# Half of the gated head outputs turned by transposing transfers instead of TensorE

## The chip, the cores and the metric

The kernel runs on one core of one Trainium2 chip. The metric is the device time of one execution in microseconds (us); lower is better. The time before is the median of three runs.

## What is computed

One layer of a hybrid decoder trunk for 512 tokens of 1024 channels, in float32. The part that matters here is branch B, a gated linear attention with 4 heads of 256 value channels, and its output gate:

```python
o = _gla_chunked(qh, kh, vh, gkh)                    # 512 tokens x 4 heads x 256
o = o * lax.rsqrt(jnp.mean(o * o, axis=-1, keepdims=True) + EPS) * gla_norm_g[l]
o = o.reshape(bsz, seq, GLA_VDIM) * jax.nn.silu(r)   # r = u @ (a part of w_in), 1024 wide
y_gla = o @ w_gla_out[l]
merged = jax.nn.sigmoid(gate_a) * y_conv + jax.nn.sigmoid(gate_b) * y_gla
```

The heads leave o with tokens on the partitions. The product with w_gla_out needs o with channels on the partitions, so the gated o, 512 tokens by 1024 channels of float32, has to be transposed.

## The kernel before

Every large product is made of three matmuls (lines 541 to 543, `mm3`): each operand is split into a high part and a low part, and low x high, high x low and high x high are added up in one PSUM bank. ScalarE (ACT) makes the high part of a weight (`whi`, line 426 or 456) and VectorE (DVE) the low part (`wlo`, line 427 or 464). Weights come as tiles of 512 KB into four `raw` buffers. SyncE's queue (SP) issues nearly all of these loads, in an order that is fixed when the program is built, and each load waits until the buffer it overwrites has been read. Tokens come in four tiles p of 128; channels of o in two halves n of 512 (two heads each) or in eight tiles m of 128.

Every engine works through its own list in order. A scheduler builds the lists from the program text and its own estimates, so an instruction that waits holds up everything behind it on its engine.

The stretch around the change has four pieces, in this order.

1. *The heads.* Class `Head` leaves the normalised output in `ot[p, n]` (called `h` in the trace), 128 tokens x 512 channels.
2. *The product for r.* `seven("w_r", ...)` computes u @ w_r by the seven-product scheme of Strassen and Winograd, in the steps a11, a12, s1, n2, s4, n3, a22, each with two products of 24 matmuls in all. Four of the steps complete two blocks (p, n) each: a12 blocks (0,0) and (1,0); s4 blocks (0,1) and (1,1); n3 blocks (2,1) and (3,1); a22 blocks (2,0) and (3,0). `put_r` applies the silu on ACT (line 1555 or 1550) into a tile `r`, and DVE then multiplies `ot[p, n]` by it (line 1561, the last one at 1565), one block late.
3. *The turning.* `gated_o(m, bank)` (lines 1246 to 1259) turns one channel tile: four TensorE transposes of 128x128 (line 1250) into one PSUM bank `ax`, one ACT instruction that scales it into the high part (line 1257), one DVE instruction that makes the low part (line 1258). Their results are `oa[m]`; tiles m = 0 to 3 are called `oa` in the trace and 4 to 7 `h`. The eight calls come in pairs: (4,5) at the end of the product for r, (6,7), (0,1) and (2,3) inside the next piece.
4. *Gate B, tiles 6 and 7.* `two_tiles` (lines 1344 to 1382) makes two column tiles of gate B at once, in four quarters x1, x3, x2, x4 of 24, 24, 24 and 12 matmuls 256 wide. A sum of weight pieces for x3 and x4 is made on GpSimd (POOL, `two_sums`, line 398). The quarters accumulate into three banks x, y and z, and after a part of the sum is complete ACT copies it out (line 1351) before the next quarter goes on in the same bank. So x3 cannot begin on bank x before ACT has copied what x1 left there. The pairs of turned tiles stand after x1, x3 and x2. Behind x4 comes the product with w_gla_out (`tile_of("w_gla", m, ...)`), which needs all eight `oa`.

Of the kernel before, what the change touches and what calls it, by code (L numbers as in the profile page):

```python
# [12 lines left out]
BF16 = mybir.dt.bfloat16  # L13
U8 = mybir.dt.uint8
AF = mybir.ActivationFunctionType
ALU = mybir.AluOpType

P = 128
D = 1024
T = 512  # L20
# [80 lines left out]
def trunk_layer(ctx: ExitStack, tc: tile.TileContext, a: dict, out: bass.AP):  # L101
# [15 lines left out]
    tp = pool("temps", 1)  # L117
    ps = pool("psum", 1, bass.MemoryType.PSUM)
    edge = ctx.enter_context(tc.tile_pool(name="edge", bufs=1, side="right"))
    heap_scope, hp = scoped("heap", 26)  # L120
# [9 lines left out]
    def heap(dt=F32):  # L130
        return hp.tile([P, T], dt, tag="h", name=nm("h"))
# [143 lines left out]
    ready, raws = [], []  # L275
    pair_raws = {}
    kept = {}
# [136 lines left out]
    def split_weight(halves=False, between=None):  # L414

        if len(ready) < len(order):
# [4 lines left out]
            if name in SEVEN or name == "two":  # L421
# [3 lines left out]
                lo = wp.tile([P, D], F32R, tag="wlo", name=nm("wlo"), bufs=4)[:, :n]  # L425
                nc.scalar.copy(hi, raw)  # L426
                two_low[:] = [nc.vector.tensor_tensor(lo, raw, hi.bitcast(F32), ALU.subtract)]  # L427
# [817 lines left out]

    def gated_o(m, bank):
        po = bank()
        c = (m % 4) * P
        for p in range(NT):
            nc.tensor.transpose(po[:, p * P : (p + 1) * P], ot[p, m // 4][:, c : c + P], ident)  # L1250
        gain = pp[:, PP_GG + m % 2 : PP_GG + m % 2 + 1]
        if m < 3:
            both = tp.tile([P, 2, T], F32R, tag="x", name=nm("oa"), bufs=3)
        elif m == 3:
            both = tp.tile([P, 2, T], F32R, tag="gain", name=nm("oa"), bufs=1)
        hi, lo = (both[:, 0, :], both[:, 1, :]) if m < 4 else (heap(F32R), heap(F32R))
        nc.scalar.activation(hi, po, AF.Copy, scale=gain)
        low_at[:] = [nc.vector.scalar_tensor_tensor(lo, po, gain, hi.bitcast(F32), ALU.mult, ALU.subtract)]
        oa[m] = hi, lo

# [279 lines left out]
    def sums_for(step):  # L1540
        while urgent and step in ("s1", "n2", "s4", "n3") and step not in merge_acts:
            urgent.pop(0)[1]()

    def put_r(step, t, n, acc):
        if step in ("a11", "s1", "n2"):
            rt[t, n] = rp_.tile([P, T], F32, tag="r", name=nm("r"), bufs=6)
            return nc.scalar.copy(rt[t, n], acc)
        if step == "a22":
            rt[t, n] = rp_.tile([P, T], F32, tag="r", name=nm("r"), bufs=6)
            nc.scalar.activation(rt[t, n], acc, AF.Silu)  # L1550
        else:
            r = rt[t, n]
            one, two = (r, acc) if step == "n3" else (acc, r)
            done = nc.vector.tensor_tensor(r, one, two, ALU.add if step == "a12" else ALU.subtract)
            nc.scalar.activation(r, r, AF.Silu)
        if step == "a22":
            done = None
        with tc.issue_after(done.ins) if done else ExitStack():
            while gated:
                i, j = gated.pop()  # L1560
                nc.vector.tensor_tensor(ot[i, j], ot[i, j], rt[i, j], ALU.mult)
        gated.append((t, n))
        if (step, t, n) == ("a22", 3, 0):
            i, j = gated.pop()
            nc.vector.tensor_tensor(ot[i, j], ot[i, j], rt[i, j], ALU.mult)
        return done if step == "n3" else None

    def r_at(step, i):
        if (step, i) == ("a22", 1):
            for m in range(4, 6):  # L1570
                gated_o(m, ax_bank)

    seven("w_r", R_PAIRS, [ByTile(k) for k in range(4)], None, r_at, put=put_r, before=sums_for)
    half_of = [range(KT // 2), range(KT // 2, KT)]
# [4 lines left out]
    def pair_7(n):  # L1579
# [5 lines left out]
        for j in range(4):  # L1585
# [6 lines left out]
            if n == 0 and j < 3:  # L1592
                for m in ((6, 7), (0, 1), (2, 3))[j]:
                    gated_o(m, ax_bank)
                if j == 2:
                    start_norms()
# [425 lines left out]
```

## Time and profile before

| | |
|---|---|
| median of the three runs | 817.39 us (817.36 to 818.07) |
| the profiled execution, its own time | 816.96 us |
| its span in the trace | 815.3 us |
| TensorE (PE) busy | 807.5 us, 99% |
| VectorE, ScalarE, GpSimd busy | 700.7, 487.9, 192.5 us |
| the 32 transposes of line 1250 | start at 284.2 to 296.2 us |
| the eight scalings of line 1257 on ScalarE | 284.9 to 297.1 us, about 0.68 us each |
| the eight low parts of line 1258 on VectorE | 286.5 to 298.9 us, about 0.74 us each |

In a row of the trace the first number is the start in us from the span's start, the second the duration, then engine, line, operation, and the tiles as written tile <- read tiles. A name in brackets at the end is what ended the engine's idle time before it. Instructions of one engine overlap a little at their ends, so the distance between two starts is less than the duration. SPq is the queue of SyncE, where a transfer is issued; the time that a transfer takes until its data has landed is given with the DMA issues.

### The profile page before, as it was taken

How to read it: one execution, taken by the hardware profiler on the slowest of the kernel's cores; microseconds unless marked ns; L12 is line 12 of the kernel's file. 1: busy time of each engine (PE TensorE's matmuls, PEld its weight loads, DVE VectorE, ACT ScalarE, POOL GpSimd, SP SyncE). 2: the span in 40 equal slices, each digit the busy share in tenths (PEclk: the TensorE clock that was granted, in tenths of full speed). 3: DMA queues.
4: the chain of work that ended last, by engine and by line, in shares of the span. 5: the costliest groups of instructions: out<-in, count | busy, mean ns of one | idle time of the engine just before them, and what ended most of it. 6: DMA issues, size and time to landing. Idle time of an engine off the chain costs nothing.

```text
span 815.3 us, 11441 instructions
## 1 busy us (share of the span) xinstructions
PE 807.5 (99%) x4215; PEld 693.2 (85%) x4215; DVE 700.7 (86%) x1108; ACT 487.9 (60%) x746; POOL 192.5 (24%) x166
## 2 busy tenths in 40 slices
PE   9999999999999999999999999999999999999996
PEld 7888888788888898989888898898889988899885
DVE  6679999998998988486779899979976999789896
ACT  6667788677546575494435655556435663466655
POOL 2025433332204332122001100320133300522010
PEclk9999999999999999999999999999999999999999
DMA  8487858745831232432458613145732345334662
GB/s 337 146 198 179 187 160 176 161 119 135 186 95 60 78 130 78 137 105 95 164 124 220 190 57 126 52 154 156 144 127 92 142 117 167 105 104 171 165 129 105
DMA packets 36616, 113.60 MB, mean 139 GB/s; under 512 B 3704, under 2 KB 8960, under 8 KB 36560
## 3 DMA queue, kind: packets, MB, share of 16 engines
q1 hardware_dynamic: 29200, 86.92, 30.8%
q0 software_dynamic: 7200, 25.69, 18.0%
q8 instruction: 33, 0.54, 0.3%
q14 instruction: 23, 0.19, 0.1%
q10 hardware_dynamic: 160, 0.27, 0.1%
HBM read 110.76 MB, written 2.10 MB: 138 GB/s over the span
## 4 chain that ended last, share of the span: by engine, by line
PE 84%; DVE 13%; issue 1%; ACT 1%; DMA 1%; SPq 0%; DVEq 0%; ACTq 0%
PE mm L541 20%; PE mm L542 20%; PE mm L543 20%; DVE c L902 5%; PE cv L541 4%; PE cv L542 4%; PE cv L543 4%; DVE aside L902 3%; PE ax L542 2%; PE ax L541 2%; PE ax L543 2%; PE ax L1230 1%; PE ax L1232 1%; DMA kept<-in_w_r_dram 1%; PE ax L1212 0%
## 5 line engine op out<-in xcount | busy, mean ns | idle before, releaser
L541 PE MATMUL mm<-uh,wlo 128*128 128x512 f32 (+1 forms) x532 | 193.9, 364 | 0.2 <-DVE wlo L464 0.2
L542 PE MATMUL mm<-ul,whi 128*128 128x512 f32 (+1 forms) x532 | 191.6, 360 | 0.0
L543 PE MATMUL mm<-uh,whi 128*128 128x512 f32 (+1 forms) x532 | 191.4, 360 | 0.0
L427 DVE TENSOR_TENSOR wlo<-raw,whi 128x1024 fp32r<-128x1024 f32 x82 | 96.0, 1178 | 36.0 <-ACT whi L426 32.2
L398 POOL TENSOR_TENSOR raw<-raw,raw 128x512 f32<-128x512 f32 x39 | 63.9, 1638 | 236.3 <-DVE wlo L427 130.9
L541 PEld LDWEIGHTS mm<-uh,wlo 128*128 128x128 f32 x532 | 100.5, 189 | 15.6 <-DVE wlo L464 0.6
L543 PEld LDWEIGHTS mm<-uh,whi 128*128 128x128 f32 x532 | 100.4, 189 | 15.4
L542 PEld LDWEIGHTS mm<-ul,whi 128*128 128x128 f32 x532 | 100.5, 189 | 14.7
L426 ACT CAST whi<-raw 128x1024 fp32r<-128x1024 f32 x82 | 78.9, 965 | 41.4 <-PE mm L543 24.4
L456 ACT CAST whi<-raw 128x1024 fp32r<-128x1024 f32 x80 | 83.5, 1048 | 27.5 <-PE mm L543 13.9
L464 DVE TENSOR_TENSOR wlo<-raw,whi 128x1024 fp32r<-128x1024 f32 x50 | 66.3, 1331 | 7.1 <-ACT whi L456 6.8
L426 ACT CAST whi<-kept 128x1024 fp32r<-128x1024 f32 (+1 forms) x40 | 40.1, 1008 | 32.4 <-DVE kept L374 16.5
L902 DVE SCALAR_TENSOR_TENSOR aside<-cv,pp,aside 128x255 f32<-128x255 f32 (+6 forms) x112 | 52.2, 466 | 0.0
L902 DVE SCALAR_TENSOR_TENSOR c<-aside,btmp,c 128x247 f32<-128x247 f32 (+13 forms) x93 | 52.1, 565 | 0.0
L427 DVE TENSOR_TENSOR wlo<-kept,whi 128x1024 fp32r<-128x1024 f32 (+1 forms) x40 | 47.5, 1191 | 4.9 <-ACT whi L426 4.7
L902 DVE SCALAR_TENSOR_TENSOR c<-cv,pp,c 128x247 f32<-128x247 f32 (+13 forms) x93 | 43.2, 465 | 1.4 <-ACT c L898 1.4
L458 ACT ACTIVATE wlo<-raw 128x1024 fp32r<-128x1024 f32 x28 | 29.4, 1059 | 19.1 <-PE mm L541 19.1
L1351 ACT COPY tmp<-mm 128x256 f32<-128x256 f32 x38 | 14.1, 370 | 35.1 <-PE mm L543 34.3
L1733 DVE SCALAR_TENSOR_TENSOR tmp<-mm,pp,tmp 128x511 f32<-128x511 f32 (+1 forms) x42 | 31.2, 743 | 3.5 <-ACT tmp L1730 3.4
L1733 DVE SCALAR_TENSOR_TENSOR tmp<-tmp,pp,tmp 128x511 f32<-128x511 f32 (+1 forms) x32 | 27.8, 888 | 0.3
L1504 DVE TENSOR_TENSOR hres<-hres,mm 128x512 f32<-128x512 f32 (+1 forms) x37 | 24.7, 676 | 2.2 <-PE mm L543 2.1
L542 PE MATMUL cv<-ul,whi 128*128 128x512 f32 (+1 forms) x72 | 25.6, 356 | 0.0
(514 smaller groups left out, 2078.3 us busy)
## 6 DMA issues: line engine op xcount, KB each, us to landing
raw<-in_w_up_dram SPq DMA_DIRECT2D x44, 512.0 KB, 3.2
raw<-in_w_glu_dram SPq DMA_DIRECT2D x16, 512.0 KB, 5.1
raw<-in_w_down_dram SPq DMA_DIRECT2D x16, 512.0 KB, 3.4
wlo<-in_w_glu_dram POOLq DMA_DIRECT2D x12, 512.0 KB, 7.1
kept<-in_w_down_dram POOLq DMA_DIRECT2D x9, 512.0 KB, 5.5
raw<-in_w_v_dram SPq DMA_DIRECT2D x8, 512.0 KB, 6.0
raw<-in_w_qk_dram SPq DMA_DIRECT2D x8, 512.0 KB, 6.3
raw<-in_w_gb_dram SPq DMA_DIRECT2D x8, 512.0 KB, 4.0
```

The source lines that it names most:

```text
L398: work = nc.gpsimd.tensor_tensor(out, x, y, ALU.add)
L426: nc.scalar.copy(hi, raw)
L427: two_low[:] = [nc.vector.tensor_tensor(lo, raw, hi.bitcast(F32), ALU.subtract)]
L456: nc.scalar.copy(hi, raw)
L458: pace[0] = nc.scalar.mul(lo, raw, -1.0)
L464: pace[0] = nc.vector.tensor_tensor(lo, raw, hi.bitcast(F32), ALU.subtract)
L541: nc.tensor.matmul(acc, ll, rh, start=first, stop=False, **kw)
L542: nc.tensor.matmul(acc, lh, rl, start=False, stop=False, **kw)
L543: nc.tensor.matmul(acc, lh, rh, start=False, stop=last, **kw)
L902: nc.vector.scalar_tensor_tensor(out[:, j:], x[:, : half_t - j], w, out[:, j:], ALU.mult, ALU.add)
L1504: done = nc.vector.tensor_tensor(hres[t, n][:, c], hres[t, n][:, c], acc[:, c], op)
L1733: nc.vector.scalar_tensor_tensor(z[:, s:], acc[:, : T - s], w[j], z[:, s:], ALU.mult, ALU.add)
```

## The change

The tokens of tiles p = 0 and 1 (half of the gated o, whose blocks are gated earliest) no longer go through TensorE. When such a block has been gated, ACT copies its 16 bit words, low halves and high halves apart, over the `r` tile that has just been used (`words`), and SP's queue writes them to a buffer in DRAM as rows of 16 bit words, two rows for each token. When both blocks of a half n are written, SP's queue reads them back by a transfer that transposes 16 bit words (`turn_o`): one of 512x512 words for n = 0 and two of 512x256 for n = 1. The two words of a float32 come to lie side by side again, so the landing holds 256 tokens of float32 with channels on the partitions. The landings take the place of a loaded weight (`rx`) and of two `r` tiles.

The transposes of tiles p = 2 and 3 stay on TensorE, two channel tiles to a bank (`gated_two`). The scaling and the low part are now made in halves of 256 tokens (`half_o`), from PSUM for the later tokens and from the landing for the earlier ones. For tiles 4 to 7 the halves out of the landing stand one pair of calls later than those out of PSUM. All these halves are ordered behind the last silu, or behind the low parts of earlier tiles, and the first high parts of gate B's weights are ordered behind the last copied words.

```diff
+    dram = pool("dram", 1, bass.MemoryType.DRAM)
...
-                nc.scalar.copy(hi, raw)
+                with tc.issue_after(behind_planes[0].ins) if behind_planes and spec[0] == "w_gb" else ExitStack():
+                    nc.scalar.copy(hi, raw)
...
-    def gated_o(m, bank):
+    last_silu = []
+    turned, words_of = {}, [dram.tile([T, DV * 2], U16, name=nm("words")) for _ in range(2)]
+
+    def words(t, n):
+
+        planes = rt[t, n].bitcast(U16).rearrange("p (two c) -> p two c", two=2)
+        behind_planes[:] = [nc.scalar.copy(planes, ot[t, n].bitcast(U16).rearrange("p (c two) -> p two c", two=2))]
+        rows = words_of[n][2 * t * P : 2 * (t + 1) * P, :]
+        nc.sync.dma_start(rows.rearrange("(p two) c -> p two c", two=2), planes)
+
+    def turn_o(n):
+        if n == 0:
+            landings = [rp_.tile([P, 4, H], F32, tag="rx", name=nm("turned"), bufs=1)]
+        else:
+            landings = [rp_.tile([P, 2, H], F32, tag="r", name=nm("turned"), bufs=6) for _ in range(2)]
+        many = 4 // len(landings)
+        for i, landing in enumerate(landings):
+            c = slice(i * many * P, (i + 1) * many * P)
+            nc.sync.dma_start(landing.bitcast(U16), words_of[n][:, c], transpose=True)
+            for j in range(many):
+                turned[4 * n + i * many + j] = landing[:, j, :]
+
+    def gated_two(m, bank):
         po = bank()
-        c = (m % 4) * P
-        for p in range(NT):
-            nc.tensor.transpose(po[:, p * P : (p + 1) * P], ot[p, m // 4][:, c : c + P], ident)
-        gain = pp[:, PP_GG + m % 2 : PP_GG + m % 2 + 1]
+        for j in range(2):
+            c = (m % 4 + j) * P
+            for p in (2, 3):
+                at = j * H + (p - 2) * P
+                nc.tensor.transpose(po[:, at : at + P], ot[p, m // 4][:, c : c + P], ident)
+        for j in range(2):
+            start_o(m + j)
+            if m < 4:
+                half_o(m + j, slice(0, H), turned[m + j], last_silu)
+            half_o(m + j, slice(H, T), po[:, j * H : (j + 1) * H], last_silu)
+        if m < 4:
+            for j in range(2):
+                half_o(m + 4 + j, slice(0, H), turned[m + 4 + j], low_at)
...
-        nc.scalar.activation(hi, po, AF.Copy, scale=gain)
-        low_at[:] = [nc.vector.scalar_tensor_tensor(lo, po, gain, hi.bitcast(F32), ALU.mult, ALU.subtract)]
-        oa[m] = hi, lo
+        oa[m] = (both[:, 0, :], both[:, 1, :]) if m < 4 else (heap(F32R), heap(F32R))
+
+    def half_o(m, c, x, behind_op):
+        (hi, lo), gain = oa[m], pp[:, PP_GG + m % 2 : PP_GG + m % 2 + 1]
+        with tc.issue_after(behind_op[0].ins):
+            nc.scalar.activation(hi[:, c], x, AF.Copy, scale=gain)
+            low = nc.vector.scalar_tensor_tensor(lo[:, c], x, gain, hi[:, c].bitcast(F32), ALU.mult, ALU.subtract)
+        if m < 4:
+            low_at[:] = [low]
...
+    def gate_o(t, n):
+        nc.vector.tensor_tensor(ot[t, n], ot[t, n], rt[t, n], ALU.mult)
+        if t < 2:
+            words(t, n)
+        if t == 1:
+            turn_o(n)
...
-                i, j = gated.pop()
-                nc.vector.tensor_tensor(ot[i, j], ot[i, j], rt[i, j], ALU.mult)
+                gate_o(*gated.pop())
         gated.append((t, n))
         if (step, t, n) == ("a22", 3, 0):
-            i, j = gated.pop()
-            nc.vector.tensor_tensor(ot[i, j], ot[i, j], rt[i, j], ALU.mult)
+            gate_o(*gated.pop())
+            gated_two(4, ax_bank)
...
-                for m in ((6, 7), (0, 1), (2, 3))[j]:
-                    gated_o(m, ax_bank)
+                gated_two((6, 0, 2)[j], ax_bank)
```

The program's lists change at two places that matter. The first is ScalarE at the end of the product for r, from the silu of block (1,1) to the high parts of gate B's first two weights. Before:

```order
L1555 ACTIVATE r_2599<-r_2599 128x512
L1555 ACTIVATE r_2545<-r_2545 128x512
L426 CAST whi_2683<-raw_2644 128x1024
L426 CAST whi_2691<-raw_2687 128x1024
L1555 ACTIVATE r_2559<-r_2559 128x512
L1550 ACTIVATE r_2708<-cv_2412 128x512
```

The same place after (the `h` are gated blocks, `r` the used gate tiles, `raw_2656` and `raw_2705` the weights of x1 and x3):

```order
L1603 ACTIVATE r_2605<-r_2605 128x512
L1255 COPY r_2591<-h_2129 128x1024
L1603 ACTIVATE r_2551<-r_2551 128x512
L1255 COPY r_2605<-h_2131 128x1024
L429 CAST whi_2701<-raw_2656 128x1024
L1603 ACTIVATE r_2565<-r_2565 128x512
L429 CAST whi_2709<-raw_2705 128x1024
L1598 ACTIVATE r_2726<-cv_2416 128x512
```

The two copies of words of half n = 1 now stand ahead of both high parts, and one silu stands between these. The second place is ScalarE a little later, from the last silu to the high part of the first weight of w_gla_out. Before:

```order
L1550 ACTIVATE r_2741<-mm_2413 128x512
L1257 ACTIVATE h_2728<-ax_2723,pp 128x512
L426 CAST whi_2800<-raw_2687 128x512
L1257 ACTIVATE h_2737<-ax_2732,pp 128x512
L1351 COPY tmp_2748<-mm_2745 128x256
L456 CAST whi_2848<-raw_2754 128x1024
```

After (`turned_2632` is the landing of the first transposing transfer, `turned_2682` that of the second):

```order
L1598 ACTIVATE r_2741<-mm_2417 128x512
L1297 ACTIVATE h_2750<-ax_2745,pp 128x256
L429 CAST whi_2808<-raw_2705 128x512
L1297 ACTIVATE oa_2845<-turned_2632,pp 128x256
L1297 ACTIVATE oa_2850<-turned_2632,pp 128x256
L1297 ACTIVATE h_2754<-ax_2745,pp 128x256
L1392 COPY tmp_2761<-mm_2758 128x256
L1297 ACTIVATE h_2750<-turned_2682,pp 128x256
L1297 ACTIVATE h_2754<-turned_2682,pp 128x256
L459 CAST whi_2859<-raw_2767 128x1024
```

The copy of x1's sum out of bank x (`tmp_2761<-mm_2758`) now stands behind two halves out of the first landing, and the copies that follow it behind halves out of the second and third. On SP's list the four writes and the three transposing transfers come in among the weight loads. Before, from the loads for gate B on:

```order
L292 DMA raw_2644<-in_w_gb_dram 128x1024
L292 DMA raw_2645<-in_w_gb_dram 128x1024
L296 DMA raw_2754<-in_w_gla_dram 128x1024
L296 DMA raw_2804<-in_w_gla_dram 128x1024
L292 DMA raw_2852<-in_w_ga_dram 128x1024
```

After:

```order
L1257 DMA words_1285<-r_2452 128x1024
L294 DMA raw_2656<-in_w_gb_dram 128x1024
L294 DMA raw_2657<-in_w_gb_dram 128x1024
L298 DMA raw_2767<-in_w_gla_dram 128x1024
L1257 DMA words_1285<-r_2466 128x1024
L1267 DMA_TRANSPOSE turned_2632<-words_1285 128x4x512
L1257 DMA words_1286<-r_2591 128x1024
L1257 DMA words_1286<-r_2605 128x1024
L1267 DMA_TRANSPOSE turned_2682<-words_1286 128x2x512
L1267 DMA_TRANSPOSE turned_2683<-words_1286 128x2x512
L298 DMA raw_2812<-in_w_gla_dram 128x1024
L294 DMA raw_2863<-in_w_ga_dram 128x1024
```

One write stands ahead of the loads for gate B, and three writes and all transposing transfers between the first and the second load for w_gla_out.

More of the change, by code (lines that the diff above doesn't have):

```diff
@@ L14 @@
 U8 = mybir.dt.uint8
+U16 = mybir.dt.uint16
 AF = mybir.ActivationFunctionType
@@ L275, in trunk_layer @@
     ready, raws = [], []
-    pair_raws = {}
+    pair_raws, behind_planes = {}, []
     kept = {}
@@ L1244, in trunk_layer, with start_o @@
     ot = {}
-    def gated_o(m, bank):
-        po = bank()
-        c = (m % 4) * P
-        for p in range(NT):
-            nc.tensor.transpose(po[:, p * P : (p + 1) * P], ot[p, m // 4][:, c : c + P], ident)
-        gain = pp[:, PP_GG + m % 2 : PP_GG + m % 2 + 1]
+    last_silu = []
[17 more added lines that the diff above has]
+    def gated_two(m, bank):
+        po = bank()
+        for j in range(2):
[11 more added lines that the diff above has]
+                half_o(m + 4 + j, slice(0, H), turned[m + 4 + j], low_at)
+    def start_o(m):
         if m < 3:
@@ L1255, in gated_o @@
             both = tp.tile([P, 2, T], F32R, tag="gain", name=nm("oa"), bufs=1)
-        hi, lo = (both[:, 0, :], both[:, 1, :]) if m < 4 else (heap(F32R), heap(F32R))
-        nc.scalar.activation(hi, po, AF.Copy, scale=gain)
-        low_at[:] = [nc.vector.scalar_tensor_tensor(lo, po, gain, hi.bitcast(F32), ALU.mult, ALU.subtract)]
-        oa[m] = hi, lo
+        oa[m] = (both[:, 0, :], both[:, 1, :]) if m < 4 else (heap(F32R), heap(F32R))
[6 more added lines that the diff above has]
+            low_at[:] = [low]
     part = [None] * KT
@@ L1549, in put_r @@
             rt[t, n] = rp_.tile([P, T], F32, tag="r", name=nm("r"), bufs=6)
-            nc.scalar.activation(rt[t, n], acc, AF.Silu)
+            last_silu[:] = [nc.scalar.activation(rt[t, n], acc, AF.Silu)]
         else:
@@ L1559, in put_r @@
             while gated:
-                i, j = gated.pop()
-                nc.vector.tensor_tensor(ot[i, j], ot[i, j], rt[i, j], ALU.mult)
+                gate_o(*gated.pop())
         gated.append((t, n))
         if (step, t, n) == ("a22", 3, 0):
-            i, j = gated.pop()
-            nc.vector.tensor_tensor(ot[i, j], ot[i, j], rt[i, j], ALU.mult)
+            gate_o(*gated.pop())
+            gated_two(4, ax_bank)
         return done if step == "n3" else None
-    def r_at(step, i):
-        if (step, i) == ("a22", 1):
-            for m in range(4, 6):
-                gated_o(m, ax_bank)
-    seven("w_r", R_PAIRS, [ByTile(k) for k in range(4)], None, r_at, put=put_r, before=sums_for)
+    seven("w_r", R_PAIRS, [ByTile(k) for k in range(4)], None, put=put_r, before=sums_for)
     half_of = [range(KT // 2), range(KT // 2, KT)]
@@ L1592, in pair_7 @@
             if n == 0 and j < 3:
-                for m in ((6, 7), (0, 1), (2, 3))[j]:
-                    gated_o(m, ax_bank)
+                gated_two((6, 0, 2)[j], ax_bank)
                 if j == 2:
```

## The prediction

> **What bounds the kernel now.** I read the page's head first, then the busy time by stretches, the waits of TensorE (PE), and the chain of waits.
>
> ```profile
> span 815.3 us, 11441 instructions
> ...
> PE 807.5 (99%) x4215; PEld 693.2 (85%) x4215; DVE 700.7 (86%) x1108; ACT 487.9 (60%) x746; POOL 192.5 (24%) x166
> ```
> ```profile
> 250.00:284.00 34.00, 33.88 (x150) 27.76 (x149) 31.93 (x30) 21.74 (x28) 11.02 (x7) 1.00 0.18 62
> 284.00:303.00 19.00, 19.00 (x142) 17.99 (x141) 15.73 (x19) 14.41 (x23) 6.44 (x4) 1.00 0.35 112
> 303.00:800.00 497.00, 496.97 (x2756) 434.59 (x2755) 418.66 (x555) 267.00 (x380) 98.32 (x73) 1.00 0.44 129
> ```
> ```profile
> PEld mm L542 <- DVE wlo L427: 0.7, 2, 0.5
> ```
>
> The windows give length, then busy time of PE, its weight loads, DVE, ACT and POOL. In the stretch of the turning (284 to 303) PE is busy for all of 19.00 us, and for 496.97 of the next 497.00. The third row is all the waiting that the list of waits shows for PE or its weight loads from 280 us to the end: 0.7 us. So a microsecond of PE work taken out at 284 arrives at the end whole, and one of waiting put in arrives whole too. The granted clock is 1.00 in all three windows. In the first, the product for r, ACT is busy for 21.74 us of 34.00.
>
> The time of the turning itself is in the chain of waits, where each row is start, duration, engine and line:
>
> ```profile
> 284.33 0.87 PE ax L1250 x8
> ...
> 288.08 0.87 PE ax L1250 x8
> ...
> 295.56 0.87 PE ax L1250 x8
> ...
> 464.08 0.43 PE ax L622 x4
> ```
>
> These are the first, the second and the last of four groups: all 32 transposes are on the chain, 0.87 us for each eight. The last row is another set of transposes of the same size, four alone: 0.43. So the cost goes with the number, 0.109 us each, and there is no fixed part that halving a group would keep.
>
> **What goes.** 16 transposes leave, four from each group: 16 x 0.109 = **1.74 us** less on PE. 0.2% of 817.39 us is 1.63 us, which is about what a measurement of this kernel can tell from no change. So the whole gain stands only just above that line, and a wait of a tenth of a microsecond puts it below.
>
> **What comes to ScalarE (ACT), and whom it delays.** Four copies of 128x1024 words come in. These rows show what ACT, DVE and POOL do where they stand:
>
> ```profile
> 275.67 0.63 ACT L1555 ACTIVATE r<-r 128x512 f32<-128x512 f32 x1 [1.46 <-DVE r L1554]
> 278.51 0.63 ACT L1555 ACTIVATE r<-r 128x512 f32<-128x512 f32 x1 [2.20 <-DVE r L1554]
> 279.05 1.99 ACT L426 CAST whi<-raw 128x1024 fp32r<-128x1024 f32 x2
> 280.94 0.62 ACT L1555 ACTIVATE r<-r 128x512 f32<-128x512 f32 x1
> 281.65 0.60 ACT L1550 ACTIVATE r<-cv 128x512 f32<-128x512 f32 x1
> 283.14 1.05 ACT L426 CAST whi<-raw 128x1024 fp32r<-128x1024 f32 x1 [0.89 <-PE mm L543]
> 284.37 0.60 ACT L1550 ACTIVATE r<-mm 128x512 f32<-128x512 f32 x1 [0.18 <-PE mm L543]
> 284.87 0.68 ACT L1257 ACTIVATE h<-ax,pp 128x512 fp32r<-128x512 f32 x1
> 285.44 0.62 ACT L426 CAST whi<-raw 128x512 fp32r<-128x512 f32 x1
> 285.95 0.70 ACT L1257 ACTIVATE h<-ax,pp 128x512 fp32r<-128x512 f32 x1
> 286.68 0.37 ACT L1351 COPY tmp<-mm 128x256 f32<-128x256 f32 x1
> ...
> 290.42 0.37 ACT L1351 COPY tmp<-mm 128x256 f32<-128x256 f32 x1
> 290.69 0.62 ACT L1060 CAST sum<-btmp 128x512 fp32r<-128x512 f32 x1
> ```
> ```profile
> 271.00 1.81 DVE L1561 TENSOR_TENSOR h<-h,r 128x512 f32<-128x512 f32 x1
> ...
> 275.57 1.18 DVE L1561 TENSOR_TENSOR h<-h,r 128x512 f32<-128x512 f32 x1
> ...
> 278.40 0.68 DVE L1561 TENSOR_TENSOR h<-h,r 128x512 f32<-128x512 f32 x1
> ...
> 280.20 2.35 DVE L427 TENSOR_TENSOR wlo<-raw,whi 128x1024 fp32r<-128x1024 f32 x2
> 282.47 1.28 DVE L1561 TENSOR_TENSOR h<-h,r 128x512 f32<-128x512 f32 x2
> ...
> 288.43 0.41 DVE L1354 TENSOR_TENSOR tmp<-tmp,mm 128x256 f32<-128x256 f32 x1
> ```
> ```profile
> 282.63 2.26 POOL L398 TENSOR_TENSOR raw<-raw,raw 128x512 f32<-128x512 f32 x1 [6.44 <-DVE wlo L427]
> ...
> 305.81 1.29 POOL L398 TENSOR_TENSOR raw<-raw,raw 128x512 f32<-128x512 f32 x1 [2.22 <-DVE wlo L427]
> ```
>
> No row shows a copy of 16 bit words. It writes 1024 elements a partition, like the cast at 283.14 (1.05 us), and moves the bytes of a 512 wide silu (0.60). I take 1.05, with 0.60 and twice the cast, 2.1, as ends. The third copy, of block (0,1), waits for its gating to end at 275.57 + 1.18 = 276.75 and lies in the idle 2.20 us ahead of 278.51. The first two lie in such waits too: they stand in the window in which ACT idles for 12 us, and only SyncE's queue waits for them. The fourth is not hidden: block (1,1) is gated at 278.40 + 0.68 = 279.08, so it ends at 280.15, and the two casts that began at 279.05 come behind it, with the silu of 280.94 now between them. Walked on in the new order, ends overlapping by 0.1: cast to 281.1, silu to 281.65, cast to 282.6. On DVE the first `wlo` then ends at 282.3 (2.35 / 2 each), a gating at 282.9, the second `wlo` at 284.05, where it ended at 282.55.
>
> POOL's sum waits for that second `wlo` (its row says so) and moves from 282.63 to 284.1, ending at 286.4. The cast `whi<-raw 128x512` reads the sum. Before, POOL was done at 284.89 and the cast went at 285.44 unhindered. Now ACT reaches it at 285.4, waits about 1.0 us, and casts from 286.45. Behind it on ACT stand two halves from the first landing, one from PSUM, and then the copy of x1's sum, which PE needs before x3. A 256 wide step takes 0.37, and the next can start 0.27 after its start (290.42 to 290.69); the 512 wide cast at 285.44 holds ACT for 0.51 (to the next row, 285.95). So 286.45 + 0.51 + 3 x 0.27 = 287.77, ending at 288.14; PE sees it at 288.2.
>
> PE's side is in its own timeline:
>
> ```profile
> 284.17 1.03 PE L1250 MATMUL ax<-ident,h 128*128 128x128 f32 x8
> ...
> 287.92 1.04 PE L1250 MATMUL ax<-ident,h 128*128 128x128 f32 x8
> 288.71 0.36 PE L541 MATMUL mm<-hq,wlo 128*128 128x256 f32 x1
> ```
>
> From 284.17 to 287.92 is one group and x1: 3.75, of which 3.75 - 0.87 = 2.88 are x1. With four transposes it is 3.75 - 0.435 = 3.315, and the next four take 0.435, so x3 wants to begin at 287.92. It waits until 288.2: **0.28 us lost**. With a copy of 0.60 the wait is nothing; with 2.1 everything is 1.35 later and it is 1.6. After that the same walk finds room: x3 and its four transposes end at 288.2 + 2.88 + 0.435 = 291.5, when x2 wants bank x; what x3 left there is complete half way, at 289.7, and ACT copies it near 290.1.
>
> The scalings and low parts double in number at half width: ACT 16 x 0.37 against 8 x 0.68, +0.5 us; DVE 16 x 0.41 against 8 x 0.74, +0.7. DVE's 15.73 us of 19.00 become 16.4 of 17.3, so it still fits, with about 0.8 us of cover. If that is gone, the low parts of the first w_gla_out tile are late and PE waits there.
>
> **SyncE's queue and the transfers.** These rows are the price list:
>
> ```profile
> raw<-in_w_up_dram SPq DMA_DIRECT2D x44, 512.0 KB, 3.2
> ...
> wlo<-in_w_gb_dram POOLq DMA_DIRECT2D x6, 512.0 KB, 8.9
> ...
> out_dram<-hres SPq DMA_DIRECT2D x2, 256.0 KB, 2.0
> ...
> out_dram<-y ACTq DMA_DIRECT2D x1, 256.0 KB, 2.7
> ```
> ```profile
> 270.49 14.76 SPq L296 DMA_DIRECT2D raw<-in_w_gla_dram  x2
> ```
>
> A write of 256 KB lands in 2.0 to 2.7 us; I take 2.3. The second copy follows the gating that ends at 271.00 + 1.81 = 272.81 and ends at 273.9, so the first transposing transfer is issued at 276.2. The last write is issued at 280.2, and the other two transfers at 282.5 or behind the first. Call X the time in which 512 KB land transposed; no row shows it. A plain load of 512 KB lands in 3.2 at best, the slowest row of that size, an adding transfer from another queue, says 8.9. I take 4, since this is a plain move on SP's queue. Then the first lands at 280.2 (wanted at 286.96) and the third at 286.5 (wanted at 290.7 by ACT's list, and up to 292.2 before PE stops: x2's second half wants bank y at 291.5 + 1.44 = 292.96, and two halves and a copy stand ahead of that on ACT, 0.75). Nothing waits. The second load for w_gla_out, queued behind all this, was issued only at 270.49 + 14.76 = 285.25 before, when POOL had read its buffer; POOL's delay takes it to 286.5 and SP is free by 283. Landed 4 us later, at 290.5, it is ahead of its cast, which stands behind the third landing's halves.
>
> If X is above 6.3, the last write queues behind the first transfer and the third lands at about 276.9 + 2X. That passes 292.2 at X = 7.65; from there each microsecond of X costs two.
>
> The Trainium skill speaks against the change here: VectorE: DVE Perf Modes, section The three transpose paths, gives 1309 ns for one 128x128 tile of 2 bytes by transfer, 390 by TensorE, and advises TensorE where PSUM will do. The same skill, DMA: Bandwidth & Descriptors, section Latency and other measured facts, gives 261 GB/s, an estimate of 2.0 us for 512 KB. No run here shows which. By the first, if the 32 tiles go one after another, an estimate of X is 21 us and of the time about 843; by the second my sum stands.
>
> **Sum.** For the profiled execution 816.96 - 1.74 + 0.28 = 815.50 us. The median of the runs is 0.43 above that execution: **815.9 us**.
>
> **Rivals.**
> 1. *All of the gain.* The fourth copy is short, or POOL's sum takes less (1.29 in the row at 305.81), and ACT is in time: 817.39 - 1.74 = 815.65, faster by 0.21%. For it: only 0.28 us separate the two. Against it: each link of that walk is in order on its engine. Chance 0.28.
> 2. *Late landings, slower.* The transfer of 16 bit words is slow; the waiting engine is ACT, in order, with the copies out of banks x and y behind it, so PE stops in x2. X = 10, a little above the slowest row, puts the third landing at 296.9, 4.7 late: 815.9 + 4.7 = 820.6. It makes the kernel slower by 0.2% from X = 9.2. For it: it moves words of 2 bytes, where the plain loads move rows of 4 KB (512 KB over 128 partitions). Against it: all plain rows of 512 KB. Chance 0.17. Of that, 0.03 stand for the Trainium skill's first figure above, tile after tile.
> 3. *The copies cost more than they hide.* At 2.1 us each, or X near 8, PE loses 1 to 3 us: 816.7 to 818.6, no change to be seen. Chance 0.10.
>
> That PE does not lose the transposes is excluded: its list has 4017 rows before and 4001 after.
>
> **How the numbers follow.** The forecast has 0.45. Faster is rival 1, 0.28; slower is rival 2 and a little of 3, 0.19; no change 0.53. The low end is rival 1 less a quarter of a microsecond, a third of the spread of the three runs: 815.4; the high end takes in rival 3 and X up to 8.9 (1.0 us above the median, 818.4), 818.6.
>
> **What would show it.** Right: PE without idle time from 284 but for some 0.3 us at the start of x3, released by the copy out of bank x; ACT waiting for POOL ahead of the 512 wide cast; the transposing transfers landing in 3 to 6 us. Wrong: ACT waiting for a landing, SP's later loads issued after 288, or the transposes' group of four taking more than 0.44.

## The result and the profile after

The changed kernel takes 820.68 us (median of 7 runs, 819.19 to 821.13), the kernel before, run beside it, 817.39 (817.19 to 818.11, 7 runs): ratio 1.0034 [1.0023, 1.0046]. (The ratios here are estimates over all runs, with a 95% interval, and not the quotient of two medians, which is 1.0040.) By the medians it is slower by 3.3 us. The forecast was 815.9, with 818.6 as the high end. The profiled execution of the changed kernel took 820.93 us.

The head of its page, and the same three windows as before (length, then busy time of PE, weight loads, DVE, ACT and POOL, then the granted clock):

```profile
span 819.1 us, 11443 instructions
...
PE 808.3 (99%) x4199; PEld 692.8 (85%) x4199; DVE 704.2 (86%) x1116; ACT 492.9 (60%) x758; POOL 191.5 (23%) x166
```
```profile
250.00:284.00 34.00, 33.71 (x149) 27.51 (x148) 30.46 (x30) 25.22 (x32) 10.22 (x6) 1.00 0.35 109
284.00:303.00 19.00, 16.26 (x119) 14.84 (x117) 17.66 (x26) 15.93 (x31) 6.18 (x4) 1.00 0.48 139
303.00:800.00 497.00, 496.52 (x2744) 434.00 (x2745) 418.62 (x555) 263.73 (x373) 98.66 (x73) 1.00 0.45 129
```

Ahead of 284 ACT has 3.5 us more than before, the copies of words, and PE is busy for 0.17 us less. From 284 to 303 PE, which had no gap there, now stands for 2.74 of 19.00 us. From 303 on it stands for 0.48, and the first 0.45 of these are the end of the same wait. The list of its waits from 250 us on says for whom (us in total, times, longest):

```profile
PE mm L545 <- DVE oa L1298: 2.5, 1, 2.5
PE mm L544 <- ACT tmp L1392: 0.7, 1, 0.7
PE cv L544 <- DVE r L1602: 0.3, 1, 0.3
```

The second row is the wait at x3 that the prediction named. The first is the one that it did not price: a low part out of `half_o` (L1298) is late for the first tile of w_gla_out. PE's timeline shows all of it:

```profile
284.61 0.60 PE L1277 MATMUL ax<-ident,h 128*128 128x128 f32 x4
287.91 0.60 PE L1277 MATMUL ax<-ident,h 128*128 128x128 f32 x4
289.18 0.39 PE L544 MATMUL mm<-hq,wlo 128*128 128x256 f32 x1 [0.67 <-ACT tmp L1392]
...
297.34 0.40 PE L544 MATMUL mm<-oa,wlo 128*128 128x512 f32 x1
...
300.31 0.39 PE L544 MATMUL mm<-oa,wlo 128*128 128x512 f32 x1
300.54 0.39 PE L545 MATMUL mm<-oa,whi 128*128 128x512 f32 x1
303.45 0.50 PE L545 MATMUL mm<-oa,whi 128*128 128x512 f32 x1 [2.52 <-DVE oa L1298]
...
304.15 0.63 PE L544 MATMUL mm<-h,wlo 128*128 128x512 f32 x1
...
307.43 0.39 PE L546 MATMUL mm<-h,whi 128*128 128x512 f32 x1
```

At 297.34 the changed kernel begins the tile 0.36 us *ahead* of the kernel before (297.70): up to here the change has gained. Matmuls follow each other every 0.23 us, so the one due at 300.77 comes at 303.45, 2.68 us late. And then the matmuls take 0.63 where they took 0.39, until 307. Two windows of one microsecond show why; the third number from the end is the granted clock:

```profile
302.00:303.00 1.00, 0.00 (x0) 0.00 (x0) 1.00 (x2) 0.00 (x0) 1.00 (x1) 1.00 0.00 0
...
305.00:306.00 1.00, 1.00 (x4) 0.81 (x3) 0.41 (x1) 0.00 (x0) 0.00 (x0) 0.50 0.68 274
```

After the idle stretch the clock is 0.50 for some 3 us; windows of 0.1 us put this from 303.85 to 307.27. From 303.45 to 307.43 are ten matmuls in 3.98 us; at 0.229 each (297.34 to 300.54 is fourteen steps in 3.20) they would be 2.29: 1.69 us lost. So 2.68 + 1.69 - 0.36 = 4.01 us against before, and the two profiled executions differ by 820.93 - 816.96 = 3.97.

Why the low part is late stands on DVE's timeline:

```profile
296.98 1.22 DVE L467 TENSOR_TENSOR wlo<-raw,whi 128x1024 fp32r<-128x1024 f32 x1
298.11 0.48 DVE L1298 SCALAR_TENSOR_TENSOR oa<-ax,pp,oa 128x256 fp32r<-128x256 f32 x1
298.50 2.29 DVE L430 TENSOR_TENSOR wlo<-raw,whi 128x1024 fp32r<-128x1024 f32 x1
300.71 2.29 DVE L467 TENSOR_TENSOR wlo<-raw,whi 128x1024 fp32r<-128x1024 f32 x1
302.93 0.47 DVE L1298 SCALAR_TENSOR_TENSOR oa<-ax,pp,oa 128x256 fp32r<-128x256 f32 x1
```
```profile
298.41 3.50 POOL L400 TENSOR_TENSOR raw<-raw,raw 128x512 f32<-128x512 f32 x2 [12.14 <-DVE wlo L467]
301.88 2.25 POOL L400 TENSOR_TENSOR raw<-raw 128x512 f32<-128x512 f32 x1
```

Between the last half of tile 2 (298.11) and that of tile 3 (302.93) stand two weight low parts, and each takes 2.29 us in place of the 1.22 of the row above them, while POOL's sums run beside them. In the kernel before, DVE did the first of these two weights ahead of both low parts of `oa`, and the second behind both.

The transfers did what was forecast. In the list of DMA issues (count, KB, median us to landing):

```profile
words<-r SPq DMA_DIRECT2D x4, 256.0 KB, 2.0
...
turned<-words SPq DMA_TRANSPOSE x3, 4.0
```

The later load for w_gla_out is issued at 286.30, and no engine waits for a landing.

### The profile page after: what moved, and what is told of

It reads as the page before. It is cut to its first block, busy times and chain, and to the rows that moved or that the text cites. A ratio compares the mean times of both kernels' runs of the same rounds, so it can differ in the third digit from the quotient of the medians.

```text
span 819.1 us, 11443 instructions
## 1 busy us (share of the span) xinstructions
PE 808.3 (99%) x4199; PEld 692.8 (85%) x4199; DVE 704.2 (86%) x1116; ACT 492.9 (60%) x758; POOL 191.5 (23%) x166
## 4 chain that ended last, share of the span: by engine, by line
PE 83%; DVE 14%; issue 1%; ACT 1%; DVEq 0%; ACTq 0%
PE mm L544 19%; PE mm L545 19%; PE mm L546 19%; DVE c L905 5%; PE cv L545 4%; PE cv L544 4%; PE cv L546 4%; DVE aside L905 3%; PE ax L546 2%; PE ax L544 2%; PE ax L545 2%; DVE wlo L430 1%; PE mm L761 1%; PE ax L1233 1%; PE ax L1235 1%
## 5 line engine op out<-in xcount | busy, mean ns | idle before, releaser
L430 DVE TENSOR_TENSOR wlo<-raw,whi 128x1024 fp32r<-128x1024 f32 x82 | 99.4, 1218 | 35.5 <-ACT whi L429 31.6
L467 DVE TENSOR_TENSOR wlo<-raw,whi 128x1024 fp32r<-128x1024 f32 x50 | 65.8, 1321 | 7.1 <-ACT whi L459 6.9
```

Source lines behind the costliest of these rows:

```text
L467: pace[0] = nc.vector.tensor_tensor(lo, raw, hi.bitcast(F32), ALU.subtract)
```

## The experiments

The theory (A) after the comparison: transfers and copies cost nothing, the transposes' 1.74 us are gained, and all is given back and more by one wait of PE for DVE, made by the *order* of DVE's list and by POOL's sums beside it, plus the clock that falls behind the wait. The rival (B): the added work itself, the copies on ACT and the transfers' traffic, makes the neighbourhood late, and the wait is only where that shows.

**The weight low parts put behind the last half.** The changed kernel, with one edit of order:

```diff
+                with tc.issue_after(last_low[0].ins) if last_low and spec[0] == "w_ga" else ExitStack():
+                    two_low[:] = [nc.vector.tensor_tensor(lo, raw, hi.bitcast(F32), ALU.subtract)]
...
+                with tc.issue_after(last_low[0].ins) if last_low and (name, spec) == ("w_gla", 2) else ExitStack():
+                    pace[0] = nc.vector.tensor_tensor(lo, raw, hi.bitcast(F32), ALU.subtract)
...
+            if m == 2:
+                last_low[:] = [low]
```

> Theory A (the loss is VectorE's list: the last half low parts stand behind two weight low parts, which GpSimd's sums slow to 2.29 us each; TensorE waits 2.5 us for the half of tile 3, and its clock is halved for 3 us after): with the half low parts ahead, the one for tile 3 ends near 300 us, TensorE waits under 0.5 us there, the granted clock stays at 1.00, and the time is 816.2 to 816.9 us. Rival B (the copies of words and the transposing transfers cost the time, through memory traffic or SyncE's queue): nothing changes, 819 to 821. Rival C (the halves cost too much work on ScalarE and VectorE, wherever they stand): the wait moves to another low part, 818 or more.

Measured: 816.61 us (815.92 to 817.32, 11 runs; before 817.32), ratio 0.9990 [0.9981, 0.9999]. DVE's timeline of this kernel:

```profile
298.27 0.48 DVE L1302 SCALAR_TENSOR_TENSOR oa<-ax,pp,oa 128x256 fp32r<-128x256 f32 x1
299.43 0.48 DVE L1302 SCALAR_TENSOR_TENSOR oa<-ax,pp,oa 128x256 fp32r<-128x256 f32 x1 [0.68 <-ACT oa L1301]
299.83 1.92 DVE L1302 SCALAR_TENSOR_TENSOR h<-turned,pp,h 128x256 fp32r<-128x256 f32 x2
301.68 1.78 DVE L1066 TENSOR_TENSOR sum<-btmp,sum 128x512 fp32r<-128x512 f32 x1
```

The last half is done at 299.9, PE doesn't wait there, the clock stays, and 4.1 us are back. All copies and transfers are still in: B is refuted for the main loss, and so is C of that text, the halves' mere amount of work; the order of the list is shown as a cause. DVE even stands idle for 0.68 us ahead of that half, because ACT's high part is not there yet: that is the gap which the weight low parts had been put into. POOL's sums now hit other operations: the `sum` of 512 takes 1.78 (0.68 alone).

**POOL's sums held back.** The changed kernel in its own order, but POOL's sums for gate A's pair wait for a copy of one column out of the last half low part:

```diff
+        if part == "x1" and name == "w_ga" and last_low:
+            seen = small(1, "var")
+            held = nc.gpsimd.tensor_copy(seen, last_low.pop()[:, H : H + 1].bitcast(F32))
+            with tc.issue_after(held.ins):
+                two_sums_now(name, p, q, part, add, left, right)
+            return
...
```

> VectorE's list is left as it is; GpSimd's three sums for the next pair wait until the half low part of tile 3 is made (a one-column copy holds them). Theory A with GpSimd as a part of the cause: the two weight low parts take 1.2 us each in place of 2.3, the half of tile 3 ends near 301.2, TensorE waits about 0.4 us, the clock stays at 1.00: 816.5 to 817.2 us. If the order alone is the cause and GpSimd none: the wait stays near 2 us or more, 818.5 or more. Rival B: 819 to 821.

Measured: 817.31 us (817.02 to 818.05, 11 runs), ratio 0.9999 [0.9990, 1.0008], just above the 816.5 to 817.2 expected. DVE's timeline:

```profile
299.19 1.22 DVE L439 TENSOR_TENSOR wlo<-raw,whi 128x1024 fp32r<-128x1024 f32 x1
300.33 1.22 DVE L476 TENSOR_TENSOR wlo<-raw,whi 128x1024 fp32r<-128x1024 f32 x1
301.46 0.48 DVE L1307 SCALAR_TENSOR_TENSOR oa<-ax,pp,oa 128x256 fp32r<-128x256 f32 x1
```

The same two weight low parts in the same place take 1.22 each, and PE waits 0.4 us. So without POOL's sums the wait is shorter by 2 x 1.07 us, and without the order it is gone: the long wait takes both, and either remedy alone removes most or all of it.

**A PSUM bank for each turned tile.** In the changed kernel two tiles share a bank, so that ACT's half of the second waits until DVE has read the first:

```diff
-        po = bank()
+        po = [bank() for _ in range(2)]
...
-                at = j * H + (p - 2) * P
-                nc.tensor.transpose(po[:, at : at + P], ot[p, m // 4][:, c : c + P], ident)
+                at = (p - 2) * P
+                nc.tensor.transpose(po[j][:, at : at + P], ot[p, m // 4][:, c : c + P], ident)
...
```

> Each turned tile gets a PSUM bank of its own, where the change lays two into one. Theory D (in one bank ScalarE's second half waits until VectorE has read the first; that is what makes x3 late by 0.7 us and the low parts late): ScalarE has no wait for VectorE in the turning, x3 begins 0.3 to 0.7 us earlier, the half low part of tile 3 is made before the weight low parts, TensorE waits under 0.5 us: 815.8 to 816.6 us. Rivals B and C: 818.5 or more.

Measured: 816.13 us (815.73 to 816.69, 11 runs), ratio 0.9986 [0.9978, 0.9995]. PE's waits of over 0.1 us from 250 us on, all of them:

```profile
PE cv L544 <- DVE r L1602: 0.3, 1, 0.3
```

Both the wait at x3 and the long one are gone, without any edit of order: the scheduler itself now puts both halves ahead of the weight low parts (`oa<-ax` x2 at 296.61, the weights at 301.47 and 302.60). The shared bank is thus the first link. How it works is read from the lists and not tested by itself: it makes the last half's high part late, the list fills the gap with two weight low parts, and POOL nearly doubles these.

**Copies, writes and transposing transfers, unread.** The kernel before, with its own 32 transposes, and all that the change adds ahead of `half_o`; nothing reads the landings:

```diff
...
-                i, j = gated.pop()
-                nc.vector.tensor_tensor(ot[i, j], ot[i, j], rt[i, j], ALU.mult)
+                gate_o(*gated.pop())
```

> The kernel before with the four copies of words, the four writes and the three transposing transfers added, and their landings not read: TensorE turns everything as before. Theory A: only the first copy's delay of the steps behind it (0.4 us) and at most 0.5 us at x3 arrive: 817.7 to 818.3 us, clock at 1.00. Rival B: the loss of the change is in these, with 1.7 us of transposes on top, 820 to 822.

Measured: 817.09 us (816.71 to 818.43, 11 runs), ratio 0.9999 [0.9991, 1.0008]. The added work costs nothing that can be measured (the interval reaches 0.7 us to either side), less than A had expected and far from B's figure. B falls.

**Three waits taken away at once.** The order of the first experiment, the banks of the third, and on ACT the copy of x1's sum ahead of the halves out of the landings. Of this last part:

```diff
-                half_o(m + j, slice(0, H), turned[m + j], last_silu)
+                half_o(m + j, slice(0, H), turned[m + j], first_put)
...
+            if n == 0 and j == 0:
+                first_put[:] = put_at
```

> The changed kernel with three of its waits taken away at once: the two weight low parts stand behind the last half low part on VectorE, each turned tile has its own PSUM bank, and the copy of x1's sum stands ahead of the halves out of the landings on ScalarE. If those waits are all that stands between the changed kernel and the sixteen transposes' worth, 817.3 - 1.74 = 815.6, with up to 0.4 us left for the later start of the turning: 815.6 to 816.0, TensorE without a wait of over 0.3 us from 284 to 304. If something else takes the gain (the copies, the transfers), it stays at 816.1 or above, like the kernel with two banks alone.

Measured: 816.14 us (815.34 to 816.45, 11 runs), ratio 0.9985 [0.9976, 0.9993]. That is no better than a bank for each tile alone: the other two edits bring nothing that can be measured once the banks are apart. The upper of the expected cases held. A part of the rest shows in PE's timeline: the second group of transposes takes 0.94 us (0.96 with two banks alone) where the others take 0.60.

```profile
284.78 0.60 PE L1279 MATMUL ax<-ident,h 128*128 128x128 f32 x4
288.08 0.94 PE L1279 MATMUL ax<-ident,h 128*128 128x128 f32 x4
```

**The first copy of words moved.** In nearly all the profiles with the copies the product for block (3,1) starts late, 279.04 in the changed kernel against 278.62, and a first copy that delays the cast behind it could be why.

```diff
-        if t < 2:
+        if (t, n) == (0, 0):
+            held_words.append(lambda: words(t, n))
+        elif t < 2:
             words(t, n)
...
+        if step == "s1" and t == 3:
+            held_words.pop()()
```

> The kernel before it, and the first copy of words moved behind the last gated block's silu, so that the cast behind it on ScalarE is not delayed. If that copy makes the gate product's end late, TensorE's product for block (3,1) starts 0.4 us earlier than in the changed kernel, at about 278.6 as before, and the time falls by 0.2 to 0.4, to 815.3 to 815.7. If the later start in the changed kernel is only how executions differ, it equals the kernel before it within 0.2.

Measured: 816.00 us (815.31 to 816.38, 11 runs), ratio 0.9982 [0.9973, 0.9991], within the interval of the one before; the product still starts at 279.02. That copy is not the cause, and the theory of it falls.

**The bank of the first turned tile freed earlier.** There are three such banks, and the second group's second tile takes the first again. DVE's low part out of it stood behind the gating of block (3,0); now ahead:

```diff
-            gate_o(*gated.pop())
-            gated_two(4, ax_bank)
+            low = gated_two(4, ax_bank)
+            with tc.issue_after(low.ins):
+                gate_o(*gated.pop())
```

> The kernel with the later first copy, and on VectorE the low part of the first turned tile put ahead of the gating of block (3,0), so that its PSUM bank is free when the second group of transposes wants it. In the kernel before, that group takes 0.94 in place of 0.60 us. If this wait is the rest of what the sixteen transposes should have brought, the time falls by 0.3, to 815.6 to 815.8; if the gating is then late for the transposes of the third group, it does not fall.

Measured: 815.86 us (814.99 to 816.39, 11 runs; before 817.43), ratio 0.9979 [0.9970, 0.9988]. All four groups are now of one length:

```profile
284.60 0.60 PE L1279 MATMUL ax<-ident,h 128*128 128x128 f32 x4
287.89 0.60 PE L1279 MATMUL ax<-ident,h 128*128 128x128 f32 x4
291.21 0.60 PE L1279 MATMUL ax<-ident,h 128*128 128x128 f32 x4
294.52 0.60 PE L1279 MATMUL ax<-ident,h 128*128 128x128 f32 x4
```

It is the fastest version, with 1.57 of the 1.74 us of the sixteen transposes. The step from the kernel ahead of it (0.14 us, of 0.3 expected) is smaller than the intervals, so that the time alone does not show it.

**The clock: waits of other lengths.** The changed kernel and four others ask what the lowered clock hangs on. First the changed kernel itself once more.

> The changed kernel unaltered, for more of its times. If the lowered clock behind the wait of 2.7 us is a cause of its own, the times fall into two groups 1.6 us apart, 819.2 with a mean clock of 0.998 and 820.5 to 821.1 with 0.996; if the clock follows the wait always, there is one group at 820.7.

Measured: 820.63 us (818.84 to 821.11, 5 runs), ratio 1.0034 [1.0022, 1.0047]. With the first seven, twelve runs make two groups: eight from 820.46 to 821.13, whose mean granted clock is 0.996 or 0.997, and four from 818.84 to 819.24 at 0.998. Their means are 820.84 and 819.04; the 1.80 between is close to the 1.69 us of the ten slow matmuls. The two profiled runs, both of the first group, show the wait; by its time the second group has it too, without the lowered clock. So the lowered clock comes in two of three runs.

Then the same wait, shortened. Two kernels differ from the one with the sums held back only in what holds them: the first weight low part in one,

```diff
-            held = nc.gpsimd.tensor_copy(seen, last_low.pop()[:, H : H + 1].bitcast(F32))
+            held = nc.gpsimd.tensor_copy(seen, last_low.pop()[:, :1].bitcast(F32))
...
+                if spec[0] == "w_ga" and spec[-1] == "x1" and oa[3] and not first_seen:
+                    last_low[:], first_seen[:] = [lo], [1]
```

> The changed kernel, with GpSimd's three sums for gate A's pair held behind the first of the two weight low parts in place of running beside it; everything else in the same order. By the theory of the shared slowdown the first weight low part takes 1.2 us and the second still 2.2, the half low part ends about 302.4 and TensorE waits some 1.6 us in place of 2.7. If the lowered clock comes with any wait above a microsecond, the ten matmuls behind it run at half rate and the time is 819.3 to 820; if it takes a wait of nearly 3 us, the clock stays at 1.00 and the time is 818.0 to 818.5.

and the last half of tile 2 in the other:

```diff
+        if m == 2 and c.start == H:
+            last_low[:] = [lo]
```

> The changed kernel, with GpSimd's three sums for gate A's pair held behind the half low part of tile 2 by a copy of one column, so that they run beside the second weight low part and not the first; the order is otherwise the same. The first takes 1.2 to 1.7 us and the second 2.3, the last half low part ends between 302 and 302.9, and TensorE waits 1.4 to 2.2 us, between the 0.4 and the 2.7 measured so far. If the granted clock falls with a wait of this length, the time is 819.5 to 820.3 in most runs; if it takes a longer one, it stays at 1.00 and the time is 817.8 to 818.7 in all.

Measured: 817.26 us (816.88 to 817.74, 11 runs) and 817.16 (816.60 to 817.58, 11 runs), ratios 1.0000 [0.9991, 1.0009] and 0.9996 [0.9987, 1.0005]. Both missed the length of wait that they were made for: PE waits 0.4 us in each, the clock stays. The reason is in POOL's timeline of the second:

```profile
298.87 2.25 POOL L407 COPY var<-oa 128x1 f32<-128x1 f32 x1 [12.38 <-DVE oa L1307]
301.08 2.71 POOL L400 TENSOR_TENSOR raw<-raw,raw 128x512 f32<-128x512 f32 x2
```

A copy of one column takes 2.25 us while DVE does its two weight low parts at full pace (1.22 each); in the kernel with the sums held back behind the last half it takes 0.37. POOL, too, is held up by DVE, and not in proportion to its work.

At last, in the changed kernel, the second weight low part is cut in two, one piece ahead of the last half low part and one behind; with 512 columns ahead (`T`), then with 256:

```diff
+                split = last_low and (name, spec) == ("w_gla", 2)
+                if split:
+                    nc.vector.tensor_tensor(lo[:, T:], raw[:, T:], hi[:, T:].bitcast(F32), ALU.subtract)
+                c = slice(0, T) if split else slice(0, D)
+                with tc.issue_after(last_low[0].ins) if split else ExitStack():
+                    pace[0] = nc.vector.tensor_tensor(lo[:, c], raw[:, c], hi[:, c].bitcast(F32), ALU.subtract)
```

> The changed kernel, with the second weight low part cut in two on VectorE: 512 columns stay ahead of the last half low part, 512 go behind it. By the shared slowdown the half low part ends 1.1 us earlier than in the changed kernel, about 302.3; two of TensorE's matmuls stand later in its list, so that it stops 0.5 earlier, and it waits some 2.0 us. If the granted clock falls with such a wait, the time is 819.7 to 820.2; if it stays, 818.0 to 818.6. A mixture of both would put the point at which the clock falls near 2 us.

> The same with 256 columns ahead and 768 behind. The half low part ends about 301.7, three matmuls stand later, and TensorE waits some 1.6 us. With a lowered clock 819.3 to 819.8, without 817.6 to 818.2.

Measured: 821.06 us (819.12 to 821.40, 5 runs) and 820.50 (820.43 to 821.44, 5 runs; before 817.21), ratios 1.0043 [1.0028, 1.0057] and 1.0043 [1.0030, 1.0056]. Both times lie above what was expected with the lowered clock. PE waits 2.4 us in both, not 2.0 and 1.6: beside POOL a half and a quarter of the operation take 1.76 and 1.49 us, far more than a half and a quarter of 2.29. The kernel with 512 columns ahead:

```profile
298.47 2.29 DVE L431 TENSOR_TENSOR wlo<-raw,whi 128x1024 fp32r<-128x1024 f32 x1
300.68 1.76 DVE L470 TENSOR_TENSOR wlo<-raw,whi 128x512 fp32r<-128x512 f32 x1
```

And the one with 256:

```profile
300.18 1.49 DVE L470 TENSOR_TENSOR wlo<-raw,whi 128x256 fp32r<-128x256 f32 x1
```

With 0.68 for 512 alone and 1.22 for 1024, the surcharge on 512 and on 1024 columns is 1.08 and 1.07, the same for both. The lowered clock came in four of the five runs of the first and in all of the second. So no kernel here has a wait between 0.7 and 2.4 us: up to 0.7 the mean clock stayed at 0.998 or more (nine kernels, 11 runs each), from 2.4 on it fell, by mean clock and time, in 17 of 22 runs. Where between these the change lies stays open.

## Why the prediction was wrong

**What was right.** The sixteen transposes are worth what was forecast, four take 0.44 on the chain and the best version keeps 1.57 of 1.74. A copy of words takes 1.05, writes land in 2.0 and the transposing transfers in 3.7 to 4.4 us (the 512 KB of the first in 4.4), where X was taken as 4. POOL's sum ended at 286.27 (forecast 286.4) and the cast behind it began at 286.31 (286.45). The changed kernel begins w_gla_out's first tile ahead of the kernel before.

**The step that failed** is this one: "DVE's 15.73 us of 19.00 become 16.4 of 17.3, so it still fits, with about 0.8 us of cover. If that is gone, the low parts of the first w_gla_out tile are late and PE waits there." The case that it names is the one that came, and it was given no price and no chance. Three things were wrong in it.
- A sum of busy times is not a cover. DVE's new list puts two weight low parts of 1024 columns between the last halves of tiles 2 and 3; for the second of these halves what counts is what stands ahead of it. The working walks ACT's and SyncE's new lists, and DVE's only up to 284.05. The first experiment, which changes that order and little else, brings 4.1 us back.
- The halves' own price was near enough (0.47 to 0.48 long, 0.39 to the next), but POOL's sums put 1.07 us on each of the two weight low parts that run beside them. DVE was busy for 17.66 us of the 19.00, where 16.4 was forecast. The surcharge was in the trace of before, whose timeline of DVE has the same operation with and without it, and the prediction did not use it:

```profile
297.07 1.22 DVE L427 TENSOR_TENSOR wlo<-raw,whi 128x1024 fp32r<-128x1024 f32 x1
298.21 1.41 DVE L1258 SCALAR_TENSOR_TENSOR oa<-ax,pp,oa 128x512 fp32r<-128x512 f32 x2
...
300.12 2.32 DVE L464 TENSOR_TENSOR wlo<-raw,whi 128x1024 fp32r<-128x1024 f32 x1
```

- The price of a wait was taken as its length. Here 2.68 us of waiting cost 4.4, since the clock fell behind it.

In the terms of the sum, counted from row to row of PE in the two profiled executions: the transposes bring -1.74 as forecast; the wait at x3 costs 0.94 in place of 0.28; the turning starts 0.44 later (284.61 against 284.17), which the sum does not have and which is in part where the execution lies in its span (below); the wait for the low part, 2.68, and the clock behind it, 1.69, both stood at nothing. Together that is +4.01 us, where the sum had -1.46.

**The wait at x3** was forecast as 0.28 us and shows as 0.67 of idling; from the second group of transposes to the third PE takes 4.24 us, from the first to the second 3.30, so that it costs 0.94. The chain came as walked up to the cast, but the copy of x1's sum began at 288.76, not 287.77, because of a link that the walk did not have:

```profile
285.04 2.32 DVE L430 TENSOR_TENSOR wlo<-raw,whi 128x1024 fp32r<-128x1024 f32 x1
...
286.31 0.62 ACT L429 CAST whi<-raw 128x512 fp32r<-128x512 f32 x1 [0.54 <-POOL raw L400]
286.83 0.91 ACT L1297 ACTIVATE oa<-turned,pp 128x256 fp32r<-128x256 f32 x2
288.39 0.47 ACT L1297 ACTIVATE h<-ax,pp 128x256 fp32r<-128x256 f32 x1 [0.65 <-DVE h L1298]
288.76 0.36 ACT L1392 COPY tmp<-mm 128x256 f32<-128x256 f32 x1
```

The half out of PSUM waits 0.65 us for DVE, which is reading the other tile in the same bank. DVE itself comes to that tile late: the weight low part at 285.04 took 2.32 us beside POOL's sum (284.60 to 286.27). With a bank for each tile this wait and that at x3 are gone. The Trainium skill has the rule behind it: PSUM — Partial Sum Buffer, section PSUM bank collisions raise a hardware error, has two engines' accesses to one bank kept apart by software, even two reads of different columns. The trace agrees, with 0.65 us of it.

**Rival 2** gave 820.6, and 820.68 was measured, but by another way: it needs landings of 10 us and ACT waiting for them, and they took 3.7 to 4.4 us with no wait. Its mechanism is refuted, and the agreement of the number is chance. Of the signs listed as proof of an error none appeared either: ACT waits for no landing, the later load is issued at 286.30, a group of four takes 0.44. The list itself had the same hole as the sum, with nothing in it on DVE.

**The later start of the turning.** In the profiles of kernels with the copies the product for block (3,1) starts from 0.1 us earlier (278.52, the kernel with 256 columns ahead) to 1.1 us later than in the one of before. A part of that is only how the executions lie in their spans: the same operation of ACT begins at 57.62 in the changed kernel and at 57.44 in the kernel before, far ahead of the change. Counted from the matmul ahead of it, the product comes after 0.67 to 1.02 us, in the changed kernel 0.69, where it came after 0.50. The rows show what stands in between. In the kernel before, the weight low part ahead of the step that PE waits for runs alone:

```profile
276.67 1.21 DVE L427 TENSOR_TENSOR wlo<-kept,whi 128x1024 fp32r<-128x1024 f32 x1
```

In the changed kernel, as in all with the copies, it runs beside POOL's third sum:

```profile
275.98 2.32 DVE L430 TENSOR_TENSOR wlo<-kept,whi 128x1024 fp32r<-128x1024 f32 x1
```
```profile
275.46 1.75 POOL L400 TENSOR_TENSOR raw<-raw 128x512 f32<-128x512 f32 x1
```

It is the surcharge of POOL's sums again, and moving the first copy did not alter that. The longer step, 0.18 us in the best version, is also the size of the 0.17 us that this version lacks of the transposes' 1.74. No run took it away, so that this cause is read from the rows and not shown by experiment.

## What to carry over

Busy sums do not say whether an engine keeps its due times: walk the new list of each engine that PE waits for, and add to each operation the surcharge that the trace shows for it beside another engine. Two tiles in one PSUM bank tie the engines that read them together, and a scheduler may fill the gap with long work that makes the next step late; a bank for each was here nearly the whole remedy (816.13 us, the best version 815.86). Price a wait of PE of 2.4 us or more at its length and what the lowered clock adds (here 1.7).

## What the hardware did that was not expected

- *DVE beside POOL.* In the rows quoted, an operation of DVE on two SBUF operands took 1.07 to 1.10 us more beside POOL's sums, whatever its size: 1.22 became 2.29, 0.68 became 1.76 and 1.78. A surcharge that does not grow with the work fits engines that take turns, not engines that share a rate. The Trainium skill has this rule: SBUF — State Buffer, section Who interferes with whom, calls the shared port pair an exclusive lock, held for a whole instruction, which a DVE instruction with two SBUF inputs contends for and one with a single SBUF input does not. The trace agrees in the second point as well: in the kernel before, the two low parts out of PSUM (at 298.21, 1.41 for both, quoted above) ran beside POOL's sums at 0.7 each, as POOL's timeline there shows:

```profile
297.38 3.98 POOL L398 TENSOR_TENSOR raw<-raw,raw 128x512 f32<-128x512 f32 x2 [12.48 <-ACT oa L1257]
```

  The change moves half of the low parts from PSUM to a landing in SBUF, and so into that contention: a pair of them (`h<-turned`) took 1.92 beside POOL in the first experiment (one of the two 0.48, the other 1.53), and 0.88 with the sums held back:

```profile
301.86 0.88 DVE L1307 SCALAR_TENSOR_TENSOR h<-turned,pp,h 128x256 fp32r<-128x256 f32 x2
```

- *The clock.* After 2.4 to 2.5 us without a matmul PE ran at a granted clock of 0.50 in 17 of 22 runs. In windows of 0.1 us the lowered stretch is 3.41 us long in each of the four profiles that have it. It does not begin with PE's new start: in the changed kernel it begins 0.40 us after it, in the second profile of the same kernel 0.62, with 512 columns ahead 0.86, and with 256 columns ahead at 302.04, before the first matmul at 302.12. The Trainium skill, TensorE: Matmul & The Clock Gate, section What's actually happening, has the half rate come after an idle window of about 3.4 us that runs free of the program. The half rate, its being there in some runs only, the length of the lowered stretch and its begin apart from PE's start agree; the idle time does not, since an idle stretch a microsecond shorter was enough here, and the measurement decides.
